# Where the memory projection is normalised in a two-layer decoder trunk: between its last two column groups, or inside the first feed-forward block

## The chip, the cores and the metric

The kernel runs on one core of a Trainium2 chip. The metric is the device time of one execution in microseconds (us). Three executions of the kernel before took 1013.52, 1014.38 and 1016.01 us; the median is 1014.38.

## The reference, cut to what matters

The trunk has two layers over 256 tokens of width 1024. A memory of 256 rows is normalised and projected once, ahead of both layers, and both layers attend to it:

```
mem_kv = rms_norm(mem, mem_norm_g) @ mem_w_kv        # (256, 1024)
mem_k  = mem_kv[..., :512]   # 4 heads of 128, each normalised again in memory_heads
mem_v  = mem_kv[..., 512:]
for i in range(2):
    x = x + 0.5 * swiglu(rms_norm(x, ffn1_norm_g[i]), ffn1_w_in[i], ffn1_w_out[i])
    ... mixer: tokens, and memory_heads(xq, mem_k, mem_v, ...) ...
    x = x + 0.5 * swiglu(rms_norm(x, ffn2_norm_g[i]), ffn2_w_in[i], ffn2_w_out[i])
```

Two facts of `rms_norm` are used. The scale of a row is one number, so it can be applied after the projection as well as before it; the gain is applied before. And nothing reads `mem_k` and `mem_v` until the first mixer, after the whole first feed-forward block.

## The kernel before, in words

Every large product is made in three passes: an operand is split into a rounded high part and the remainder, and `mm3` (L226 to L230) issues high by high, low by high and high by low, each a 128x128x256 matmul on PE. A weight tile of 512 KB arrives by DMA in a `wr` tile (`wtile`, L218, five buffers), ACT casts it to `wh` (L213), and DVE subtracts to get `wl` (L214, eight buffers of each). A tile feeds eight calls of `mm3`, 24 matmuls.

The order of PE and of the DMA queue SP is that of the program text. The text is woven: `Weave` (L61) runs a main generator and side chains, counts modelled PE time (0.328 us for each `mm3`), and resumes a side chain when its stated delay, an entry of `LAT` (L53), has passed. If the main generator yields a condition, the side chain is run at once until the condition holds. ACT, DVE and POOL are ordered by the compiler's scheduler, which may issue an instruction ahead of its place in the text when its inputs are ready; `issue_after` (L466, L490) queues a block behind a given instruction of its engine. At run time each engine takes its instructions in order.

`memory()` (L427) is the first stage. It loads the memory in four pieces, applies the gain and splits them (`mh`, `ml`), and projects in four `Group`s of 256 columns, called here group 0 to group 3: groups 0 and 1 are keys, 2 and 3 values. Each group holds one PSUM bank and takes two weight tiles, called its first and second half.

In the kernel before, the text runs in this order. Behind the casts of group 1, ACT squares the four pieces of memory and DVE adds them (`square`, L279) and folds them (L290, L248). During group 2 the `chain` of the memory's norm follows: on PE a product with a matrix of ones (L308), on DVE two diagonals (L299), on POOL the power that gives `rc` (L313), the row scale. After group 2 the main generator waits in the text for that (`yield norm.ready`), and `head_norm` (L395) normalises the keys of groups 0 and 1, out of their banks: a square on ACT, a reduction on DVE (L401), scalings (L404, L408), a power on POOL (L406), and a product (L410). Then ACT scales the values of group 2 out of their bank into `vM` with `rc` (through `act`, L134), and the residual `x` is prepared for the feed-forward block: `x0.put` (L267) applies gains, splits, squares and sums. Only then come group 3 with its weights, and the scaling of its values. The transposed keys `kT` (L238 on PE, L451 on ACT) follow inside the first feed-forward block (`ffn_in`, L498), as does the product with ones of `x0`'s norm (L308), whose result `rb` the block needs for its first activations (`hidden`).

Of the kernel before, what the change touches and what calls it, by code (L numbers as in the profile page):

```python
# [10 lines left out]
F32 = mybir.dt.float32  # L11
# [3 lines left out]
AF = mybir.ActivationFunctionType  # L15
ALU = mybir.AluOpType
# [3 lines left out]
P = 128  # L20
# [12 lines left out]
def constants():  # L33
# [16 lines left out]

LAT = dict(pieces=1, norm=8.5, mnorm=3.5, x0=17.0, mkeys=7.2, cross=9.5, cross_s=1.5,  # L53
           cross_m=3.7, cross_p=8.7, cross_o=3.0, gates=20.0, scores=2.2, scores_m=8.4, num=6.9, num_r=7.5,
           keys=5.5, keys_d=7.2, query=9.0, head=1.5, head_m=2.5, head_p=9.3, head_o=4.0)

# [42 lines left out]
def tile_trunk(ctx: ExitStack, tc: tile.TileContext, a, out):  # L99
    nc = tc.nc  # L100
    seq = [0]

    def mk(pool, shape, dt, tag):
        seq[0] += 1
        return pool.tile(shape, dt, tag=tag, name=f"{tag}_{seq[0]}")
# [7 lines left out]
    wv = Weave()  # L113
# [19 lines left out]
    def act(*args, **kw):  # L133
        ins = nc.scalar.activation(*args, **kw)  # L134
        if args[2] not in (AF.Copy, AF.Square):
            tabled[0] = ins
# [6 lines left out]
    def unit(dt):  # L143
        return mk(up, [P, 2, T], dt, "u")

    def tmp():
        return mk(tp, [P, 2, T], F32, "t")

    def col():
        return mk(cp, [P, 16], F32, "col")  # L150

    def mo():
        return mk(pb8, [P, 512], F32, "bank")
# [7 lines left out]
    memT = [unit(F32) for _ in range(4)]  # L161
    xT = [unit(F32) for _ in range(4)]
    con = mk(cst, [P, C_END], F32, "con")
# [37 lines left out]
    def g(i):  # L201
        return gcol[:, i:i + 1]


    pieces = [1]
    last = [None]
# [11 lines left out]
    def wtile(src, nk, ncol=256):  # L218
        raw = mk(wrp, [P, nk, ncol], F32, "wr")
        nc.sync.dma_start(raw, src)  # L220
        return split(raw, [P, nk, ncol])

    def wcols(w, c0, kh):
        return wtile(w.rearrange("(k p) f -> p k f", p=P)[:, kh * 4:(kh + 1) * 4, c0:c0 + 256], 4)
# [16 lines left out]
    def split_gain(src, gc, hi, lo):  # L241
        act(hi, src, AF.Copy, scale=gc)
        nc.vector.scalar_tensor_tensor(out=lo, in0=src, scalar=gc, in1=hi.bitcast(F32),
                                       op0=ALU.mult, op1=ALU.subtract)
# [14 lines left out]
    class Norm:  # L259
# [4 lines left out]
            self.done = False  # L264
            self.xT, self.xh, self.xl = [], [], []

        def put(self, xn):  # L267
            c2 = len(self.xT)
            hi, lo = mk(xhp, [P, 2, T], F32R, "xh"), mk(xlp, [P, 2, T], F32R, "xl")
            for m in range(2):  # L270
                split_gain(xn[:, m], g(self.gi + 2 * c2 + m), hi[:, m], lo[:, m])
            self.xh.append(hi)
            self.xl.append(lo)
            self.xT.append(xn)
            self.square(xn, c2 == 0)
            if c2 == 3:
                self.fold()

        def square(self, xn, first):  # L279
            if first:  # L280
# [107 lines left out]
    def head_scales(rc, hd, scaled):  # L388

        c = mk(sp, [P, 4], F32, "qsc")  # L390
        nc.vector.scalar_tensor_tensor(out=c[:, 0:2], in0=rc, scalar=1.0 / hd, in1=rc, op0=ALU.mult, op1=ALU.mult)
        nc.vector.tensor_scalar_mul(c[:, 2:4], rc, hd ** -0.5 if scaled else 1.0)
        return c

    def head_norm(dst, src, n, hsc):  # L395

        hd = src.shape[2] // n
        sq, v, u = tmp(), col(), col()
        sqv = sq[:, :, :n * hd]
        act(sqv, src, AF.Square)  # L400
        nc.vector.tensor_reduce(out=v[:, 0:2 * n].rearrange("p (h m) -> p h m", h=2),  # L401
                                in_=sqv.rearrange("p h (m d) -> p h m d", m=n), axis=AX.X, op=ALU.add)
        for h in range(2):
            nc.vector.tensor_scalar(u[:, n * h:n * h + n], v[:, n * h:n * h + n], hsc[:, h:h + 1], EPS,  # L404
                                    op0=ALU.mult, op1=ALU.add)
        nc.gpsimd.tensor_tensor(out=u[:, 8:8 + 2 * n], in0=u[:, 0:2 * n], in1=mhalf[:, 0:2 * n], op=ALU.pow)  # L406
        for h in range(2):
            nc.vector.tensor_scalar(v[:, 8 + n * h:8 + n * h + n], u[:, 8 + n * h:8 + n * h + n],  # L408
                                    hsc[:, 2 + h:3 + h], None, op0=ALU.mult)
        tt(out=dst.rearrange("p h (m d) -> p h m d", m=n), in0=src.rearrange("p h (m d) -> p h m d", m=n),  # L410
           in1=v[:, 8:8 + 2 * n].rearrange("p (h m) -> p h m", h=2).unsqueeze(3).to_broadcast([P, 2, n, hd]),
           op=ALU.mult)

    def turn(rows):

        ps = mo()
        for m in range(2):
            for h in range(2):
                transpose(ps[:, m * T + h * P:m * T + (h + 1) * P], rows[:, h, m * P:(m + 1) * P])
        return halves(ps)  # L420
# [3 lines left out]
    vM = mk(cst, [P, 2, 512], F32, "vM")  # L424
    x0 = Norm(G_F1)

    def memory():  # L427

        idle = tmp().rearrange("p a b -> p (a b)")[:, :T].bitcast(BF16)
        nc.vector.memset(idle, 0.0)  # L430
        bank = mo()
        for i in range(WARM):
            nc.tensor.matmul(bank, idle[:, :P], idle, start=True, stop=True, skip_group_check=True)
        wkv = a["mem_w_kv"]
        mh, ml, wfirst = [], [], []
        for c2 in range(4):
            nc.sync.dma_start(memT[c2], a["memT"][:, 2 * c2:2 * c2 + 2])
            hi, lo = unit(F32R), unit(F32R)
            for m in range(2):
                split_gain(memT[c2][:, m], g(G_MEM + 2 * c2 + m), hi[:, m], lo[:, m])  # L440
            mh.append(hi)
            ml.append(lo)
            if c2 == 0:
                v = wkv.rearrange("(k p) f -> p k f", p=P)
                wfirst.append([wtile(v[:, k:k + 2, 0:256], 2) for k in (0, 2)])
            if c2 == 2:
                wfirst.append(wcols(wkv, 0, 1))
        norm = Norm(G_MEM, rows=False)

        def keys(gi, kr):  # L450
            nc.scalar.copy(kT[gi], turn(kr))  # L451
            return
            yield

        for gi in range(2):
            gr = Group(wkv, gi * 256, mh, ml, rows=True)
            for kh in range(2):
                if gi == 0 and kh == 0:
                    yield from gr.first_part(wfirst[0])
                else:  # L460
                    yield from gr.part(kh, wfirst[kh] if gi == 0 else None)
            if gi == 0:
                first = gr
                continue
            nc.sync.dma_start(con, a["con"])
            with tc.issue_after(last[0].ins):  # L466
                for c2 in range(4):
                    norm.square(memT[c2], c2 == 0)
            norm.fold()
            wv.spawn(norm.chain(), LAT['mnorm'])  # L470
            gv = Group(wkv, 512, mh, ml, rows=True)
            yield from gv.all()
            for c2 in range(4):
                nc.sync.dma_start(xT[c2], a["xT"][:, 2 * c2:2 * c2 + 2])
            yield norm.ready
            hsc = head_scales(norm.rc, P, False)
            for i, q in enumerate((first, gr)):
                kr = tmp()
                head_norm(kr, q.ps, 2, hsc)
                wv.spawn(keys(i, kr), LAT['mkeys'] + 1.5 * i)  # L480
        for gi in range(2):
            if gi == 0:
                gr = gv
            else:
                gr = Group(wkv, 768, mh, ml, rows=True)
                yield from gr.all()
            for h in range(2):
                act(vM[:, h, gi * 256:(gi + 1) * 256], gr.ps[:, h], AF.Copy, scale=norm.rc[:, h:h + 1])
            if gi == 0:
                with tc.issue_after(last[0].ins):  # L490
                    for c2 in range(4):
                        x0.put(xT[c2])
                wv.spawn(x0.chain(), LAT['x0'])


    KG = [(0, 4), (4, 4), (8, 4), (12, 4), (16, 4), (20, 2)]
# [39 lines left out]
    def ffn(x, w_in, w_out, nxt=None, mid=None):  # L536
# [13 lines left out]
        for c2 in range(4):  # L550
# [25 lines left out]
            else:  # L576
                nxt.put(xn)
        wv.spawn(nxt.chain(), LAT['norm'])

# [15 lines left out]
    def cross_spawn(gr, gi, layer, hsc, ys):  # L595
# [4 lines left out]
        def queries():  # L600
# [4 lines left out]
            for m in range(2):  # L605
                wv.spawn(head(m), LAT['cross_s'] + LAT['cross_m'] * m)
            return
            yield

        def head(m):  # L610
# [12 lines left out]
            tt(out=p, in0=p, in1=c[:, 6:8].unsqueeze(2).to_broadcast([P, 2, T]), op=ALU.mult)  # L623
            yield LAT['cross_p']
            tps = mo()
# [428 lines left out]
```

## Time and profile before

| | before |
|---|---|
| three executions, us | 1013.52, 1014.38, 1016.01 |
| span of the profiled execution, us | 1011.9 |
| median of the executions less that span, us | 2.5 |
| PE, DVE, ACT busy, us | 996.4, 673.3, 524.0 |
| mean granted clock of PE | 0.997 |

The span runs from the first to the last instruction of one profiled execution; no longer time of that execution is given. A row of the trace's timeline has the start, the duration, the engine, the line and operation, the tile written and the tiles read, and in brackets the idle time of the engine before the row with what ended it. PEld is the weight load of PE.

### The profile page before, as it was taken

To read this page: it belongs to the slowest core of one execution; us is meant where nothing else is said; L and a number is where in the kernel's file an instruction comes from. 1 tells how busy PE (TensorE), PEld (TensorE's weight loads), DVE (VectorE), ACT (ScalarE), POOL (GpSimd) and SP (SyncE) were. 2 spreads that over 40 slices of the span, in tenths; PEclk is the share of its full clock that TensorE was granted. 3 is DMA by queue.
4 is the path that set the end of the run, shared out by engine and by line. 5 is a ranking of instruction groups with operands and counts; after the bars stand their busy time and mean duration, and the time that the engine had idled before them with its cause. 6 is when DMAs were issued, how large, how long until landed. Compare 5 with 4: busy or idle time off the path is not lost.

```text
span 1011.9 us, 20587 instructions
## 1 busy us (share of the span) xinstructions
PE 996.4 (98%) x8560; PEld 978.2 (97%) x8560; DVE 673.3 (67%) x1116; ACT 524.0 (52%) x771; POOL 28.5 (3%) x27
## 2 busy tenths in 40 slices
PE   8899999999999999999999999999999999999998
PEld 7899999999999999999999999999987899999998
DVE  6876665668756786666568666656787768666551
ACT  7755444456566564454445444544557665454440
POOL 1100000000100000000000000000121000000000
PEclk9999999999999999999999999999999999999999
DMA  9676666667644566665666666566632247665650
GB/s 310 209 247 189 193 190 180 190 187 204 184 131 138 178 191 199 193 191 178 192 206 201 200 189 192 178 194 199 189 115 81 87 137 222 199 190 183 189 171 22
DMA packets 173205, 182.71 MB, mean 181 GB/s; under 512 B 7124, under 2 KB 168328, under 8 KB 173112
## 3 DMA queue, kind: packets, MB, share of 16 engines
q1 hardware_dynamic: 171872, 179.60, 58.3%
q10 hardware_dynamic: 1016, 1.58, 0.5%
q8 instruction: 67, 1.10, 0.5%
q0 software_dynamic: 224, 0.22, 0.2%
q14 instruction: 26, 0.21, 0.1%
HBM read 180.32 MB, written 1.05 MB: 179 GB/s over the span
## 4 chain that ended last, share of the span: by engine, by line
PE 92%; DVE 4%; ACT 1%; POOL 1%; DMA 1%; issue 0%; SPq 0%; POOLq 0%; ACTq 0%; DVEq 0%
PE bank L227 29%; PE bank L228 29%; PE bank L229 29%; PE bank L233 2%; DVE wl L214 1%; PE bank L238 1%; POOL col L406 1%; ACT u L134 1%; DMA wr<-in_mem_w_kv_dram 1%; PE bank L988 1%; DVE col L401 0%; DVE u L410 0%; DVE u L973 0%; DVE col L957 0%; ACT wh L213 0%
## 5 line engine op out<-in xcount | busy, mean ns | idle before, releaser
L214 DVE TENSOR_TENSOR wl<-wr,wh 128x1024 fp32r<-128x1024 f32 (+1 forms) x347 | 414.7, 1196 | 267.0 <-ACT wh L213 266.2
L213 ACT CAST wh<-wr 128x1024 fp32r<-128x1024 f32 (+1 forms) x347 | 356.9, 1031 | 391.8 <-PE bank L228 367.4
L227 PE MATMUL bank<-xh,wh 128*128 128x256 f32 x1544 | 427.8, 277 | 0.0
L228 PE MATMUL bank<-xl,wh 128*128 128x256 f32 x1544 | 426.4, 276 | 0.0
L229 PE MATMUL bank<-xh,wl 128*128 128x256 f32 x1544 | 426.4, 276 | 0.0
L227 PEld LDWEIGHTS bank<-xh,wh 128*128 128x128 f32 x1544 | 290.0, 188 | 0.1
L228 PEld LDWEIGHTS bank<-xl,wh 128*128 128x128 f32 x1544 | 289.8, 188 | 0.1
L229 PEld LDWEIGHTS bank<-xh,wl 128*128 128x128 f32 x1544 | 289.8, 188 | 0.0
L227 PE MATMUL bank<-u,wh 128*128 128x256 f32 x896 | 249.3, 278 | 0.0
L228 PE MATMUL bank<-u,wh 128*128 128x256 f32 x896 | 247.6, 276 | 0.0
L229 PE MATMUL bank<-u,wl 128*128 128x256 f32 x896 | 247.6, 276 | 0.0
L227 PEld LDWEIGHTS bank<-u,wh 128*128 128x128 f32 x896 | 168.2, 188 | 1.9 <-issue 1.7
L228 PEld LDWEIGHTS bank<-u,wh 128*128 128x128 f32 x896 | 168.3, 188 | 0.1
L229 PEld LDWEIGHTS bank<-u,wl 128*128 128x128 f32 x896 | 168.3, 188 | 0.0
L227 PE MATMUL bank<-wh,xh 128*128 128x256 f32 x208 | 60.3, 290 | 0.0
L228 PE MATMUL bank<-wl,xh 128*128 128x256 f32 x208 | 58.7, 282 | 0.0
L229 PE MATMUL bank<-wh,xl 128*128 128x256 f32 x208 | 58.5, 281 | 0.0
L503 DVE TENSOR_TENSOR t<-bank,rb 128x256 f32<-128x256 f32 x88 | 36.3, 420 | 6.7 <-PE bank L229 6.7
L227 PEld LDWEIGHTS bank<-wh,xh 128*128 128x128 f32 x208 | 39.8, 191 | 0.5 <-issue 0.3
L228 PEld LDWEIGHTS bank<-wl,xh 128*128 128x128 f32 x208 | 39.8, 191 | 0.1
L229 PEld LDWEIGHTS bank<-wh,xl 128*128 128x128 f32 x208 | 39.8, 191 | 0.0
L506 DVE TENSOR_TENSOR t<-t,bank 128x256 f32<-128x256 f32 x88 | 32.7, 413 | 0.0
(182 smaller groups left out, 671.0 us busy)
## 6 DMA issues: line engine op xcount, KB each, us to landing
wr<-in_ffn_w_in_dram SPq DMA_DIRECT2D x176, 512.0 KB, 4.3
wr<-in_ffn_w_out_dram SPq DMA_DIRECT2D x80, 512.0 KB, 3.7
wr<-in_a_w_in_dram SPq DMA_DIRECT2D x28, 512.0 KB, 3.7
wr<-in_b_w_in_dram SPq DMA_DIRECT2D x14, 512.0 KB, 4.6
wr<-in_a_w_out_dram SPq DMA_DIRECT2D x12, 512.0 KB, 3.4
wr<-in_b_w_out_dram SPq DMA_DIRECT2D x12, 512.0 KB, 3.4
wr<-in_ffn_w_out_dram SPq DMA_DIRECT2D x16, 256.0 KB, 2.9
wr<-in_mem_w_kv_dram SPq DMA_DIRECT2D x7, 512.0 KB, 7.8
```

Of the source, the lines that this page charges most:

```text
L134: ins = nc.scalar.activation(*args, **kw)
L213: last[0] = nc.scalar.copy(hi[:, i * n:(i + 1) * n], src[:, i * n:(i + 1) * n])
L214: tt(out=lo[:, i * n:(i + 1) * n], in0=src[:, i * n:(i + 1) * n], in1=hi[:, i * n:(i + 1) * n].bitcast(F32), op=ALU.subtract)
L227: nc.tensor.matmul(ps, wh, xh, start=start, stop=False, skip_group_check=True)
L228: nc.tensor.matmul(ps, wh, xl, start=False, stop=False, skip_group_check=True)
L229: nc.tensor.matmul(ps, wl, xh, start=False, stop=stop, skip_group_check=True)
L233: nc.tensor.matmul(ps, lhsT, rhs, start=start, stop=stop, skip_group_check=True)
L238: nc.tensor.transpose(ps, src, ident[:k, :k])
L406: nc.gpsimd.tensor_tensor(out=u[:, 8:8 + 2 * n], in0=u[:, 0:2 * n], in1=mhalf[:, 0:2 * n], op=ALU.pow)
L503: tt(out=t[:, m], in0=ps[m][:, :T], in1=x.rb, op=ALU.mult)
L506: tt(out=t[:, m], in0=t[:, m], in1=ps[m][:, T:], op=ALU.mult)
L988: nc.tensor.matmul(o[es[e], cs], vr[:, i, js], pTs[e][:, src], start=i == 0, stop=i == 1, skip_group_check=True)
```

## The change: what it does

The text between group 1 and group 3 is emptied. The memory's squares, its norm's chain and the two `head_norm`s leave it; no wait stands there any more. Behind each of the four groups, 4.0 us of modelled PE time after its end, ACT copies the bank unscaled: groups 0 and 1 to two tiles `raw`, groups 2 and 3 into `vM`. The gains and splits of `x` stay behind the casts of group 2, without its squares. After group 3 two chains are started: `sums` makes the squares, the fold and the chain of `x0` (first step 2.5 us into the feed-forward block), and `finish` makes those of the memory (first step at 18.0 us), scales `vM` on DVE in place, normalises the raw keys and starts their transposes. The loads keep their order.

```diff
-LAT = dict(pieces=1, norm=8.5, mnorm=3.5, x0=17.0, mkeys=7.2, ...
+LAT = dict(pieces=1, norm=8.5, mnorm=8.0, mrest=6.0, finish=18.0, raw=4.0, x0=2.5, fold=5.0, mkeys=7.2, ...

-        def put(self, xn):
+        def put(self, xn, square=True):
...
-            self.square(xn, c2 == 0)
-            if c2 == 3:
-                self.fold()
+            if square:
+                self.square(xn, c2 == 0)
+                if c2 == 3:
+                    self.fold()

-        for gi in range(2):
+        def late(raw, gr):
+            nc.scalar.copy(raw, gr.ps)
+            return
+            yield
+
+        def sums():
+            for c2 in range(4):
+                x0.square(xT[c2], c2 == 0)
+                yield 1.5
+            x0.fold()
+            yield LAT['fold']
+            yield from x0.chain()
+
+        def finish(raw):
+            for c2 in range(4):
+                norm.square(memT[c2], c2 == 0)
+                yield 2.0
+            norm.fold()
+            yield LAT['mnorm']
+            yield from norm.chain()
+            yield LAT['mrest']
+            for h in range(2):
+                nc.vector.tensor_scalar(vM[:, h], vM[:, h], norm.rc[:, h:h + 1], None, op0=ALU.mult)
+            hsc = head_scales(norm.rc, P, False)
+            for i in range(2):
+                yield 3.0
+                kr = unit(F32)
+                head_norm(kr, raw[i], 2, hsc)
+                wv.spawn(keys(i, kr), LAT['mkeys'])
+
+        raw = [unit(F32) for _ in range(2)]
+        for gi in range(4):
             gr = Group(wkv, gi * 256, mh, ml, rows=True)
             for kh in range(2):
                 if gi == 0 and kh == 0:
                     yield from gr.first_part(wfirst[0])
                 else:
                     yield from gr.part(kh, wfirst[kh] if gi == 0 else None)
-            if gi == 0:
-                first = gr
-                continue
-            nc.sync.dma_start(con, a["con"])
-            with tc.issue_after(last[0].ins):
+            dst = raw[gi] if gi < 2 else vM[:, :, (gi - 2) * 256:(gi - 1) * 256]
+            wv.spawn(late(dst, gr), LAT['raw'])
+            if gi == 1:
+                nc.sync.dma_start(con, a["con"])
+            if gi == 2:
                 for c2 in range(4):
-                    norm.square(memT[c2], c2 == 0)
-            norm.fold()
-            wv.spawn(norm.chain(), LAT['mnorm'])
-            gv = Group(wkv, 512, mh, ml, rows=True)
-            yield from gv.all()
-            for c2 in range(4):
-                nc.sync.dma_start(xT[c2], a["xT"][:, 2 * c2:2 * c2 + 2])
-            yield norm.ready
-            hsc = head_scales(norm.rc, P, False)
-            for i, q in enumerate((first, gr)):
-                kr = tmp()
-                head_norm(kr, q.ps, 2, hsc)
-                wv.spawn(keys(i, kr), LAT['mkeys'] + 1.5 * i)
-        for gi in range(2):
-            if gi == 0:
-                gr = gv
-            else:
-                gr = Group(wkv, 768, mh, ml, rows=True)
-                yield from gr.all()
-            for h in range(2):
-                act(vM[:, h, gi * 256:(gi + 1) * 256], gr.ps[:, h], AF.Copy, scale=norm.rc[:, h:h + 1])
-            if gi == 0:
+                    nc.sync.dma_start(xT[c2], a["xT"][:, 2 * c2:2 * c2 + 2])
                 with tc.issue_after(last[0].ins):
                     for c2 in range(4):
-                        x0.put(xT[c2])
-                wv.spawn(x0.chain(), LAT['x0'])
+                        x0.put(xT[c2], False)
+        wv.spawn(sums(), LAT['x0'])
+        wv.spawn(finish(raw), LAT['finish'])
 
 
     KG = [(0, 4), (4, 4), (8, 4), (12, 4), (16, 4), (20, 2)]
```

More of the change, by code (lines that the diff above doesn't have):

```diff
@@ L49 @@
 G_MEM, G_F1, G_MIX, G_F2, G_XQ, G_XK, G_AH, G_BQ, G_BK, G_END = 0, 8, 24, 40, 56, 58, 60, 68, 69, 70
-LAT = dict(pieces=1, norm=8.5, mnorm=3.5, x0=17.0, mkeys=7.2, cross=9.5, cross_s=1.5,
+LAT = dict(pieces=1, norm=8.5, mnorm=8.0, mrest=6.0, finish=18.0, raw=4.0, x0=2.5, fold=5.0, mkeys=7.2, cross=9.5, cross_s=1.5,
            cross_m=3.7, cross_p=8.7, cross_o=3.0, gates=20.0, scores=2.2, scores_m=8.4, num=6.9, num_r=7.5,
```

## The prediction

> **What bounds the kernel now.** I read the page's head and its busy table first, then PE's waits, then PE's timeline and the stages around its gaps, then ACT and DVE there.
>
> ```profile
> span 1011.9 us, 20587 instructions
> PE 996.4 (98%) x8560; PEld 978.2 (97%) x8560; DVE 673.3 (67%) x1116; ACT 524.0 (52%) x771; POOL 28.5 (3%) x27
> ```
>
> PE is the bound nearly everywhere: 1011.9 - 996.4 leaves 15.5 us without a matmul. A change that removes no matmul can win only part of these, or of matmuls run at a low clock. PE's waits say where they lie:
>
> ```profile
> PE bank L228 <- DVE wl L214: 3.0, 2, 2.1
> PE bank L227 <- ACT wh L213: 2.3, 2, 2.0
> PE bank L952 <- ACT u L134: 0.9, 1, 0.9
> PE bank L947 <- DVE u L410: 0.8, 1, 0.8
> ```
>
> The two longest waits for weight splits, 2.1 and 2.0 us, are neighbours on PE's timeline, at the start of group 3:
>
> ```profile
> 27.42 0.28 PE L229 MATMUL bank<-wh,u 128*128 128x256 f32 x1
> 29.67 0.39 PE L227 MATMUL bank<-wh,u 128*128 128x256 f32 x1 [1.97 <-ACT wh L213]
> 32.17 0.39 PE L228 MATMUL bank<-wl,u 128*128 128x256 f32 x1 [2.11 <-DVE wl L214]
> 39.34 0.28 PE L227 MATMUL bank<-xh,wh 128*128 128x256 f32 x1
> ```
>
> The row at 39.34 is the first matmul of the feed-forward block (its operand is `xh`). The stage table shows a second cost behind the gap:
>
> ```profile
> core 0: us, PE busy (x) PEld busy (x) DVE busy (x) ACT busy (x) POOL busy (x), PEclk, DMA share, GB/s
> 13.18:27.54 14.36, 14.36 (x121) 14.31 (x121) 11.20 (x22) 10.43 (x19) 0.62 (x1) 1.00 0.97 350
> 27.54:32.17 4.63, 0.55 (x4) 0.19 (x2) 3.42 (x11) 4.32 (x7) 1.45 (x2) 1.00 0.00 0
> 32.59:36.00 3.41, 3.41 (x18) 3.41 (x17) 3.24 (x6) 1.62 (x3) 1.22 (x1) 0.50 0.59 170
> 39.34:62.00 22.66, 22.66 (x201) 22.66 (x200) 20.93 (x29) 14.81 (x19) 0.00 (x0) 1.00 0.95 300
> ```
>
> From 13.18 to 27.54 PE runs unbroken, 121 matmuls in 14.36 us, 0.119 us each. In the gap it runs 4, and the DMA moves nothing. Then for 3.41 us the granted clock is 0.50 and 18 matmuls run where 29 would. Why the gap is there, ACT and DVE tell:
>
> ```profile
> 27.85 0.84 ACT L134 ACTIVATE vM<-bank,rc 128x256 f32<-128x256 f32 x2 [2.69 <-POOL rc L313]
> 28.58 1.99 ACT L213 CAST wh<-wr 128x1024 fp32r<-128x1024 f32 x2
> ```
>
> ```profile
> 26.33 0.29 DVE L299 CUSTOM_DVE_ANT_0 t<-bank,con 128x128 f32<-128x128 f32 x1 [2.33 <-PE bank L308]
> 27.85 0.16 DVE L391 SCALAR_TENSOR_TENSOR qsc<-rc 128x2 f32<-128x2 f32 x1 [0.61 <-POOL rc L313]
> 30.63 0.36 DVE L408 TENSOR_SCALAR col<-col,qsc 128x2 f32<-128x2 f32 x2 [0.91 <-POOL col L406]
> 30.89 1.22 DVE L214 TENSOR_TENSOR wl<-wr,wh 128x1024 fp32r<-128x1024 f32 x1
> 38.14 0.69 DVE L410 TENSOR_TENSOR t<-bank,col 128x512 f32<-128x512 f32 x1
> ```
>
> ACT stands 2.69 us for the row scale `rc`, which the scaling of group 2's values needs, with group 3's casts (28.58) queued behind. DVE stands for PE's product (2.33), for `rc` (0.61) and for the head norm's power (0.91), with group 3's subtraction (30.89) behind. The weights were not late:
>
> ```profile
> 15.12 0.38 SPq L220 DMA_DIRECT2D wr<-in_mem_w_kv_dram  x1
> 21.30 0.37 SPq L220 DMA_DIRECT2D wr<-in_ffn_w_in_dram  x1
> 32.14 0.37 SPq L220 DMA_DIRECT2D wr<-in_ffn_w_in_dram  x1
> ```
>
> ```profile
> wr<-in_mem_w_kv_dram SPq DMA_DIRECT2D x1, 512.0 KB, 8.1
> ```
>
> Group 3's second half was issued at 15.12 and landed 8.1 us later, at 23.2. SP itself stands from 21.30 to 32.14, because the late subtraction frees no `wr` buffer.
>
> **The change part by part.** *The gap.* If PE goes straight from group 2 to group 3, the first feed-forward matmul comes 48 matmuls (two halves of 24) after 27.54: 48 x 0.119 = 5.7, so at 33.24 in place of 39.34. That is 6.1 us: about 1.7 (half of 3.41) for the low clock, the other 4.4 for the waits and the two restarts.
>
> [...]
>
> *Are group 3's splits ready in time?* PE now wants the first half at 27.3 (two matmuls before 27.54, since the memory's product L308 leaves this place; it returns later, so the sum doesn't count it) and the second 24 matmuls, 2.85 us, later, at 30.15. What remains ahead of them is `x0.put` without squares, and up to two raw copies:
>
> ```profile
> L134 ACT ACTIVATE xh<-u,gcol x8: 493/494/506, 20.5 to 24.7; 128x256 fp32r<-128x256 f32 x8
> L243 DVE SCALAR_TENSOR_TENSOR xl<-u,gcol,xh x8: 475/482/486, 21.5 to 29.2; 128x256 fp32r<-128x256 f32 x8
> ```
>
> ```profile
> L213 ACT CAST wh<-wr 128x1024 fp32r<-128x1024 f32 x9 | 9.0, 1052 | 1.8 <-DMA wr<-in_ffn_w_in_dram 1.8
> L286 DVE TENSOR_TENSOR acc<-acc,t 128x512 f32<-128x512 f32 x3 | 2.1, 690 | 0.0
> L451 ACT COPY kT<-bank 128x512 f32<-128x512 f32 x2 | 1.2, 587 | 0.8 <-PE bank L238 0.8
> L401 DVE TENSOR_REDUCE col<-t 128x4 f32<-128x512 f32 x2 | 1.4, 678 | 0.0
> ```
>
> ```profile
> 12.51 0.91 SPq L474 DMA_DIRECT2D u<-in_xT_dram  x2
> ```
>
> ```profile
> u<-in_xT_dram SPq DMA_DIRECT2D x2, 256.0 KB, 7.0
> ```
>
> The last two pieces of `x` are issued from 12.51 and land 7.0 us later, the last by about 20.4. Eight gains of 0.494 on ACT are 4.0 us; even if none begins before 18.5 they end at 22.5. Two raw copies, priced by the copy of a bank of the same size (L451, 0.59), push that to 23.7. A cast of 1.05 and a subtraction of 1.22 (row 30.89) make the first half ready at 26.0; the second, at one subtraction more, at 27.2. Both come before PE wants them, by 1.3 and 2.9 us; without the copies the first margin is 2.5. So the whole 6.1 is taken. The copies are also the waits that the change adds: each waits on ACT for its group's last matmul, with the next casts queued behind. The text places it 4 us after that matmul, and behind it PE has the splits already made to live on.
>
> *The loads.* The moved work issues no DMA, and the order on SP is unchanged. The subtractions of group 3 at about 26 free the `wr` buffers that SP awaited until 32.14, so the feed-forward loads resume some 6 us earlier. That is as much as PE moves, and no load becomes late.
>
> *The work moved into the feed-forward block.* On ACT, four copies of 0.59 replace the four scalings of `vM`, half a bank each (0.84 for two): 0.7 us more, in an engine that is busy 14.81 of 22.66 us there. ACT feeds PE in time at that share. POOL gets the memory's powers, and is idle there (x0 in the same row). The moved DVE work is larger. By the row for L286, three sums of 0.69; two fold steps of half that size, 0.35 each; two diagonals of 0.29; two scalings of `vM`, not in the trace in this form, bounded by 0.35 (half of a 128x512 operation) and 0.69 (all of it), taken at 0.69 each; and for each head norm a reduction 0.68, four small scalings 0.7 (0.36 for two) and a product 0.69. That is 2.1 + 0.7 + 0.6 + 1.4 + 4.1 = 8.9 us. It lies between about 53 and 83 us: the chain starts 18 us of modelled time behind group 3, its last head norm stands at 18 + 8 + 8 + 6 + 3 + 3 = 46, and a modelled 0.328 is really 3 x 0.119 = 0.357. The room:
>
> ```profile
> 60.00:70.00 10.00, 10.00 (x91) 10.00 (x90) 8.24 (x13) 6.11 (x8) 0.00 (x0) 1.00 0.67 205
> 70.00:80.00 10.00, 10.00 (x90) 10.00 (x90) 6.05 (x10) 5.26 (x6) 0.00 (x0) 1.00 0.59 182
> 80.00:90.00 10.00, 10.00 (x91) 10.00 (x90) 6.76 (x9) 4.58 (x6) 0.00 (x0) 1.00 0.67 204
> ```
>
> DVE idles 1.8 + 4.0 + 3.2 = 9.0 us there, and may use up several of the eight buffered splits before PE notices. I cost it at nothing; without that cover it would be up to 8.9 us.
>
> *The new joins on PE.* Each product with ones and each set of transposes is placed in PE's fixed order, so if its operand is late, all matmuls behind it wait. Four joins are re-timed: `x0`'s product, the memory's product, two key transposes. Before, none of these held PE. The nearest rows that did are the mixer's waits of 0.9 and 0.8 at L952 and L947. The bounds are therefore 0 and 4 x 0.9 = 3.6. As nothing waited there, there is nothing to gain. I take 0.4, half of one such wait, since the stated delays leave 5 to 8 us for each.
>
> *The sum.* 6.1 - 0.4 = 5.7. The span would be 1011.9 - 5.7 = 1006.2. The median of the three runs lies 2.5 above the span; the same 2.5 gives **1008.7 us**, or 1014.38 - 5.7. From the fastest run, 1.6 above the span, it would be 1007.8. Everything later is PE's own steady work, so the gain carries to the end.
>
> **The rivals.**
>
> *The change does not do what it says: group 3's splits still come late (1013.7).* The scheduler may issue work ahead of its place in the text. It does so now:
>
> ```profile
> 1.26 0.07 DVE L826 MEMSET v<- 128x2 f32 x2
> 7.46 0.17 DVE L196 TENSOR_SCALAR nsink<-sink 128x16 f32<-128x16 f32 x1 [4.51 <-DMA sink<-in_b_sinks_dram]
> ```
>
> Both belong to the mixers, and one cost DVE 4.51 us. Nothing holds the new squares behind a cast any more. If the raw copy of group 2, which waits for its last matmul at 27.5, is put ahead of the casts, the first half is ready at 27.7 + 0.6 + 1.05 + 1.22 = 30.6, not 27.3. PE waits 3.3, the low clock takes 1.7 and the joins 0.4, and 0.7 is kept: 1013.7. If both sums (2.1 + 0.7 = 2.8 us of DVE each) run ahead of the subtraction, it is ready at 26.0 + 5.6 = 31.6, and the time is 1014.7; with one set alone 28.8, a wait of 1.5 at full clock, and 1010.2. Against it: the text places all of these behind group 3's casts.
>
> *The low clock is not in the median run (1010.4).* The waits alone give 4.4 - 0.4 = 4.0. For it: the clock row stands for one execution only, and the three times spread by 2.5 us. [...]
>
> *Slower: the head norms inside the block are too slow for their transposes (about 1018).* Before, the two head norms took from 27.85 to 38.14 + 0.69, 11.0 us, with weight splits between their steps. Now each has 7.2 modelled, 7.8 real us to its transposes. If each took 11.0, PE would wait 3.2 twice, each with a low clock of 1.7: 9.8 lost, 3.7 net, 1018.1. The gain is spent when each wait reaches 1.35 (2 x 3.05 = 6.1), a head norm of 9.2; from 2.9, or 10.7, on the change is slower by over 0.3%. Against it: two norms shared those 11.0 us, and stood in queues with group 3's starved splits.
>
> **How the numbers follow.** A measurement of this kernel can tell about 0.3%, 3 us, from no change: faster is below 1011.3, slower above 1017.4. Forecast 0.60; low clock absent 0.14; splits late 0.18, a quarter of it still below 1011.3; slower 0.08. Faster is 0.60 + 0.14 + 0.04 = 0.78, same 0.14, slower 0.08. The range starts at 1006.0: with joins that cost nothing (1008.3) and the 1.6 of the fastest run it would be 1007.4, and the three times differ by more than 1.4 among themselves. It ends at 1013.0, between the late splits' 1010.2 and 1014.7; left out are the slower case and some 0.11 of the late ones, 0.19 in all.
>
> **What would show it.** Right: no wait for `wh` or `wl` at group 3; the first `xh` matmul near 33; clock 1.00 from 32 to 36; `wr` loads at about 26; no idle time before the products with ones and the transposes. Wrong: squares of memory or `x` ahead of group 3's casts on ACT; a copy from a bank there with idle time put down to PE; a row of PE with `[... <-DVE ...]` between 45 and 90 us.

## The result, and the profile after

Eight executions of the changed kernel took 1010.63 to 1013.5 us, median 1012.8, beside a median of 1014.48 of the kernel before. The ratio, formed from all these executions (the two medians alone give 0.9983), is 0.9978, 95% interval 0.9968 to 0.9989: faster by 1.7 us between the medians, where 5.7 was forecast. The profiled execution took 1010.63 and is at the lower end; its span of 1008.8 stands against 1011.9.

```profile
span 1008.8 us, 20591 instructions
PE 994.7 (99%) x8560; PEld 976.4 (97%) x8560; DVE 673.5 (67%) x1118; ACT 525.2 (52%) x771; POOL 28.3 (3%) x27
```

PE's waits for weight splits are smaller than before, but not gone (columns as before: total, times, longest):

```profile
PE bank L227 <- ACT wh L213: 2.1, 2, 1.6
PE bank L228 <- DVE wl L214: 1.8, 2, 0.9
```

PE's timeline shows that they stand at the same place, the start of group 3:

```profile
27.15 0.28 PE L229 MATMUL bank<-wh,u 128*128 128x256 f32 x1
29.05 0.39 PE L227 MATMUL bank<-wh,u 128*128 128x256 f32 x1 [1.62 <-ACT wh L213]
30.31 0.38 PE L228 MATMUL bank<-wl,u 128*128 128x256 f32 x1 [0.87 <-DVE wl L214]
35.95 0.29 PE L227 MATMUL bank<-xh,wh 128*128 128x256 f32 x1
```

The stage table (same columns as before) has the gap and group 3 behind it, at full clock in this execution, 48 matmuls in 5.64 us:

```profile
27.27:30.31 3.04, 0.55 (x4) 0.19 (x2) 1.28 (x2) 2.85 (x4) 0.00 (x0) 1.00 0.00 1
30.31:35.95 5.64, 5.64 (x48) 5.64 (x49) 5.64 (x7) 4.99 (x7) 0.00 (x0) 1.00 0.66 193
```

The first feed-forward matmul comes at 35.95, 3.4 earlier than before (39.34), where 33 was expected. ACT's timeline says why:

```profile
16.16 0.59 ACT L457 COPY u<-bank 128x512 f32<-128x512 f32 x1 [0.97 <-PE bank L229]
16.64 2.00 ACT L213 CAST wh<-wr 128x1024 fp32r<-128x1024 f32 x2
21.81 0.59 ACT L457 COPY u<-bank 128x512 f32<-128x512 f32 x1 [3.17 <-PE bank L229]
22.30 3.31 ACT L134 ACTIVATE xh<-u,gcol 128x256 fp32r<-128x256 f32 x8
25.51 0.62 ACT L134 ACTIVATE acc<-u 128x512 f32<-128x512 f32 x1
27.46 0.59 ACT L457 COPY vM<-bank 128x512 f32<-128x512 f32 x1 [1.33 <-PE bank L229]
27.95 1.05 ACT L213 CAST wh<-wr 128x1024 fp32r<-128x1024 f32 x1
```

The raw copies (L457) stand in ACT's queue ahead of work that PE will need. Group 1's copy stands where the text has it, behind group 2's casts and ahead of the gains of `x`; but ACT runs ahead of PE, reaches it at 18.6 and waits 3.17 us for PE's last matmul of group 1, while the gains, whose inputs had landed by about 20.5 (issued by 13.40, 7.0 us to landing), stand behind it. Group 2's copy was issued ahead of its place in the text, which is behind group 3's casts; it waits 1.33 us for group 2, and group 3's first cast stands behind it. DVE is starved by the same queue, 2.75 us before the gains' remainders and 2.90 before group 3's subtraction, which ends at 30.25:

```profile
22.84 3.29 DVE L243 SCALAR_TENSOR_TENSOR xl<-u,gcol,xh 128x256 fp32r<-128x256 f32 x8 [2.75 <-ACT xh L134]
29.02 1.23 DVE L214 TENSOR_TENSOR wl<-wr,wh 128x1024 fp32r<-128x1024 f32 x1 [2.90 <-ACT wh L213]
```

SP again stands for the `wr` buffers, from 20.12 to 30.28 in place of 32.14. The rest went as the prediction expected: in the feed-forward block neither the products with ones nor the key transposes held PE, and DVE carried the moved work at 27.2 us busy of 30.

```profile
60.00:70.00 10.00, 10.00 (x91) 10.00 (x90) 9.49 (x18) 7.86 (x12) 0.00 (x0) 1.00 0.57 174
70.00:80.00 10.00, 10.00 (x91) 10.00 (x90) 9.16 (x21) 5.67 (x8) 0.72 (x1) 1.00 0.65 195
80.00:90.00 10.00, 10.00 (x90) 10.00 (x90) 8.56 (x21) 5.48 (x6) 3.49 (x3) 1.00 0.53 162
```

### The profile page after: what moved, and what is told of

Same layout as the page of the kernel before. It is cut to its first block, busy times and chain, and to the rows that moved or that the text cites. A ratio compares the mean times of both kernels' runs of the same rounds, so it can differ in the third digit from the quotient of the medians.

```text
span 1008.8 us, 20591 instructions
## 1 busy us (share of the span) xinstructions
PE 994.7 (99%) x8560; PEld 976.4 (97%) x8560; DVE 673.5 (67%) x1118; ACT 525.2 (52%) x771; POOL 28.3 (3%) x27
## 4 chain that ended last, share of the span: by engine, by line
PE 90%; DVE 4%; ACT 2%; DMA 1%; POOL 1%; issue 1%; SPq 0%; POOLq 0%; ACTq 0%; DVEq 0%
PE bank L229 29%; PE bank L227 29%; PE bank L228 29%; PE bank L233 2%; ACT u L134 1%; DVE wl L214 1%; POOL col L407 1%; PE bank L238 1%; DMA wr<-in_ffn_w_in_dram 1%; DMA wr<-in_mem_w_kv_dram 1%; ACT wh L213 1%; DVE u L985 0%; DVE col L969 0%; PE bank L1000 0%; DVE col L402 0%
```

## The experiments

Theory A: the copies' place on ACT, each waiting for PE ahead of work that PE needs, keeps the gap. Its rival, theory B: the gains, the squares or the weights' landing do. Theory C is on the spread of the times: the half clock follows a gap in some executions only.

**Group 2's copy held** behind group 3's casts.

```diff
         def late(raw, gr):
-            nc.scalar.copy(raw, gr.ps)
+            with tc.issue_after(last[0].ins):
+                nc.scalar.copy(raw, gr.ps)
```

> The raw copies are queued behind the last weight cast made when they are written; on ACT only group 2's copy moves, from ahead of group 3's casts to behind them. Theory A (group 3 is late because raw copies that wait for PE stand in ACT's queue ahead of its casts): group 1's copy still ends at 22.3 and the gains of x at 25.5, two squares follow, so group 3's first cast ends near 27.6 and its subtraction near 28.9. PE loses about 1.5 us in place of 2.9, the first xh matmul is near 34.5 in place of 35.95, and the time of a run at full clock is about 1009.2 in place of 1010.6. Theory B (the gains of x, the squares or the landing of the weights make group 3 late, whatever the copies do): the first xh matmul stays at 35.9 and the times stay as they are.

Median 1010.8 (1009.3 to 1011.2), ratio to before 0.9965 (0.9951 to 0.9978). On ACT group 1's copy stays where it was, which shows that it already stood at its place in the text, and group 2's copy now follows group 3's casts:

```profile
22.05 0.59 ACT L458 COPY u<-bank 128x512 f32<-128x512 f32 x1 [3.17 <-PE bank L229]
28.26 1.03 ACT L213 CAST wh<-wr 128x1024 fp32r<-128x1024 f32 x1
29.19 0.58 ACT L458 COPY vM<-bank 128x512 f32<-128x512 f32 x1
```

PE's timeline of the profiled execution:

```profile
27.88 0.39 PE L227 MATMUL bank<-wh,u 128*128 128x256 f32 x1 [0.21 <-ACT wh L213]
29.14 0.38 PE L228 MATMUL bank<-wl,u 128*128 128x256 f32 x1 [0.87 <-DVE wl L214]
34.77 0.28 PE L227 MATMUL bank<-xh,wh 128*128 128x256 f32 x1
```

The two waits fell from 1.62 + 0.87 to 0.21 + 0.87, the first `xh` matmul from 35.95 to 34.77. One copy of 0.59 us, moved behind two casts, was worth 1.2 us, and this execution, at full clock, took 1009.3 where 1009.2 was expected: theory A. What is left lies behind group 1's copy, as the next run shows.

**All copies held.** In addition to the edit above:

```diff
-... finish=18.0, raw=4.0, x0=2.5, ...
+... finish=18.0, raw=9.0, x0=2.5, ...
```

> The raw copies are written 9.0 in place of 4.0 us of modelled time behind their groups, and queued behind the last cast made by then, so that group 1's copy too stands behind group 3's casts. Two squares of x still stand ahead of group 3's first cast. Theory A: gains of x run from about 19 to 22.5, the first cast ends near 24.6, the subtraction near 26; PE goes from group 2 to group 3 without a wait, the first xh matmul is at 32.9, the time 1007.6 (1010.6 - 3.0), and the runs spread less, since there is no gap that could bring a low clock. Theory B: a wait of 1 us or more stays at group 3 and the time stays above 1009.5.

Median 1009.29 (1007.55 to 1009.95), ratio 0.9945 (0.9933 to 0.9958). ACT's timeline:

```profile
18.96 3.31 ACT L134 ACTIVATE xh<-u,gcol 128x256 fp32r<-128x256 f32 x8
23.22 1.04 ACT L213 CAST wh<-wr 128x1024 fp32r<-128x1024 f32 x1
```

The gains run at 18.96 in place of 22.30, group 3's first cast at 23.22 in place of 27.95, and PE waits for nothing between 14 and 60 us. Two squares of `x` still stand between gains and cast, and cost PE nothing. The first `xh` matmul of this profile is at 34.60, not at 32.9, because this execution had a stretch at half clock from 13.36 to 16.78, long before group 3:

```profile
13.36:16.78 3.42, 3.42 (x16) 3.42 (x17) 3.23 (x5) 2.30 (x3) 0.00 (x0) 0.50 1.08 388
34.60 0.28 PE L227 MATMUL bank<-xh,wh 128*128 128x256 f32 x1
```

Less the 1.5 that such a stretch costs (below), 34.60 is 33.1. The expected 1007.6 was reached by the quicker executions (1007.55, 1007.85), not by the median; that the spread would shrink was wrong, since the start has waits of its own (PE 0.60 and 0.88 us, and 12 matmuls in the 3.41 us ahead of 13.36).

**Copies and squares held.** In addition:

```diff
-                x0.square(xT[c2], c2 == 0)
+                with tc.issue_after(last[0].ins):
+                    x0.square(xT[c2], c2 == 0)
```

> As the run with all copies held, and the squares of x too are queued behind the last cast. Theory A: nothing more to win, first xh matmul at 32.9, time within 0.5 us of that run, 1007.6. If the squares ahead of group 3's casts are the cause instead, this one alone has no wait at group 3.

Median 1007.92 (1007.3 to 1009.56), ratio 0.9941 (0.9928 to 0.9953), no wait of PE between 14 and 60 us, and the first `xh` matmul at 32.27:

```profile
32.27 0.28 PE L227 MATMUL bank<-xh,wh 128*128 128x256 f32 x1
```

Its interval overlaps that of the run before, so the squares' place is not shown to matter; the copies' is. This is what the prediction had priced: 1007.9 measured, 1008.7 forecast, span 1005.7 against 1006.2.

**The residual's squares alone** moved, the memory left as before.

```diff
-                        x0.put(xT[c2])
-                wv.spawn(x0.chain(), LAT['x0'])
+                        x0.put(xT[c2], False)
+        wv.spawn(sums(), 2.5)
```

> The kernel before with only the residual's squares, fold and chain moved into the first feed-forward block, as in the change; the memory is finished between groups 2 and 3 as before. Theory A (what holds group 3 is a wait for PE or for the memory's norm ahead of its casts): nothing won, the first xh matmul at about 39, the time 1014.2 within 0.7. If the squares of x are what makes group 3 late, the gap shrinks by their 2 us and the time is about 1012.

Median 1014.82, ratio 1.0007 (0.9998 to 1.0016): nothing won. PE waits 1.97 and 2.68 us at group 3, where the kernel before waits 1.97 and 2.11, and the first `xh` matmul is at 39.97, where about 39 was expected. So the residual's squares were not what held group 3.

**The memory alone** moved, the residual's squares back in `put`.

```diff
-                        x0.put(xT[c2], False)
-        wv.spawn(sums(), LAT['x0'])
+                        x0.put(xT[c2])
+        wv.spawn(x0.chain(), LAT['x0'] + 5.0 + 6.0)
```

> The changed kernel, but with the residual's squares back in x0.put, ahead of group 3's casts, and its chain started at about the same modelled time. ACT's order then has group 1's copy (ends 22.3 as it waits for PE), eight gains, four squares, group 3's casts, and only then group 2's copy. Theory A: gains and squares take 22.3 + 3.3 + 2.5 = 28.1, the first subtraction is done at 30.4, PE loses about 3 us as in the changed kernel, first xh matmul at 36.1, time 1010.7 to 1013. If the squares cost their whole 2.5 us on top of the changed kernel's gap, the first xh matmul is at 38.4 and the time about 1014.

Median 1012.57 (1010.82 to 1014.01), ratio 0.9982 (0.9973 to 0.9991), as the whole change. Its profile has the half clock at the start, from 13.43 to 16.84, which shifts all times below by some 1.5 (1.55 was measured for a stretch, see the changed kernel again); on ACT:

```profile
23.59 0.59 ACT L457 COPY u<-bank 128x512 f32<-128x512 f32 x1 [3.17 <-PE bank L229]
29.37 1.98 ACT L213 CAST wh<-wr 128x1024 fp32r<-128x1024 f32 x2
31.55 0.57 ACT L457 COPY vM<-bank 128x512 f32<-128x512 f32 x1
```

Here group 2's copy stands behind group 3's casts, but the squares stand ahead, and PE's waits are 1.25 and 1.15 us, the first `xh` matmul at 37.62, as expected with the 1.5 added. So the residual's part of the change was worth nothing as long as a copy held ACT up: what it freed, group 2's copy took.

**Matmuls on zeros in the gap** of the changed kernel (`idle` gets a tile of its own).

```diff
             gr = Group(wkv, gi * 256, mh, ml, rows=True)
+            if gi == 3:
+                for _ in range(8):
+                    nc.tensor.matmul(bank, idle[:, :P], idle, start=True, stop=True, ...)
```

> The changed kernel with eight 128x512 bf16 matmuls on zeros (0.21 us each at full clock, 1.7 us) in PE's order ahead of group 3, inside its gap of 2.9 us; the results of these matmuls are not used. Theory C (the changed kernel's runs spread from 1010.6 to 1013.5 because the gap brings a stretch of half clock in some executions): the gap stays, the first xh matmul stays near 36.0, but the slower runs go, and the median falls from 1012.8 to about 1010.8. Rival (the spread has another cause): median and spread as in the changed kernel, or up to 0.3 us slower.

Median 1010.75, four of five executions at 1010.53 to 1010.76 and one at 1012.26. The first `xh` matmul stays late, at 36.03. The median is as expected, but the interval of the ratio (0.9955 to 0.9980) overlaps that of the changed kernel. The granted clock speaks for theory C too: its mean was 0.998 or more in all five executions, and in only six of the changed kernel's twenty (eight above, twelve below). The one at 1012.26 had 0.998 as well; a mean does not say where in the execution a stretch lies.

**The changed kernel again**, unaltered.

> The changed kernel once more, unaltered, for a second profile and more times beside the kernel before. Theory C (half clock behind its gap in some executions and not in others): times fall in two groups, 1010.6 where the gap brings no half clock and 1012 to 1013.5 where it does, and the profile, if of the upper group, shows a stretch of clock 0.50 within 5 us of 30.3 or, from the gap at the start, of 13.2. Rival: one group, or a slow profile without such a stretch before 60 us.

> The changed kernel, unaltered, for one more profile. The two profiles so far show half clock at 13.4 (one of them) and at 743 (both), and none behind the gap at group 3. [...]

> [...]

The first gave ten times of 1010.92 to 1014.01, median 1012.07, ratio 0.9975 (0.9966 to 0.9984); the other two runs took 1012.37 and 1012.26. In the profiles of the first and the last the half clock begins at 13.37 and 13.60, and the first `xh` matmul is at 37.49 and 37.60. In the second it begins behind the gap; its stage table, 3.41 us before and 3.41 from there:

```profile
26.91:30.32 3.41, 0.96 (x6) 0.55 (x5) 1.24 (x2) 2.80 (x4) 0.00 (x0) 1.00 0.01 3
30.32:33.73 3.41, 3.37 (x16) 3.37 (x16) 3.41 (x5) 3.41 (x6) 0.00 (x0) 0.50 0.51 160
```

and its timeline has:

```profile
37.50 0.29 PE L227 MATMUL bank<-xh,wh 128*128 128x256 f32 x1
```

That is 1.55 later than in the profile at full clock. Theory C holds in its first part: an execution pays some 1.5 us at the start, at group 3, or, as in the changed kernel's first profile, at neither, and which it is differs. Of the twenty executions, the six with a mean granted clock of 0.998 took 1010.63 to 1011.98 us, the fourteen with less 1011.97 to 1014.01. That times fall in two sharp groups was wrong; between 1010.6 and 1014.0 they lie nearly everywhere.

**The kernel before with matmuls on zeros**, nine ahead of group 3.

```diff
                 gr = Group(wkv, 768, mh, ml, rows=True)
+                for _ in range(9):
+                    nc.tensor.matmul(bank, idle[:, :P], idle, start=True, stop=True, ...)
```

> The kernel before, with nine matmuls on zeros ahead of group 3, inside the first part of its gap (1.9 of the 2.1 us before the first matmul of group 3); their results are not used. Theory C: the gap stays 4.6 us long, but the half clock behind it goes in most executions: 1014.2 - 1.7 = 1012.5. Rival (the half clock in the profile of before was not typical): the time stays at 1014.2.

No gain is shown: median 1013.94, ratio 0.9997 (0.9988 to 1.0005). Its profile still has the half clock, from 32.03; 2.11 us of the gap stayed empty, and the 3.41 us ahead of the stretch held 6 matmuls. But five of its eleven executions have a mean granted clock of 0.998, which none of the 51 executions of the kernel before whose clock is known reaches (0.993 to 0.997), and these five are its quickest, 1012.30 to 1013.91 us. So theory C fits about half of the executions, not most.

**Held, with matmuls on zeros in both gaps left**, on top of the kernel with copies and squares held.

```diff
+                    if gi == 0:
+                        warm(bank, 5)
                     yield from gr.part(kh, wfirst[kh] if gi == 0 else None)
...
             s = mo()
+            if layer == 1 and gi == 1 and m == 0:
+                warm(s, 10)
```

> The kernel with copies and squares held, with matmuls on zeros in the two gaps of PE that are left: five in the start, ahead of the second half of group 0, ten in the second layer's cross attention, ahead of the first scores of its second pair of heads (0.21 us each at full clock, 1.1 and 2.1 us); their results are not used. Theory C (each gap of about 2 us can bring 3.4 us of half clock, depending on the execution): all executions at full clock, time 1006.0 to 1006.5 in each, against 1007.3 to 1009.6. Rival (the spread has another cause): median 1007.9 and the same spread; or the idle matmuls delay the real ones, and it is slower.

Median 1008.28 (1007.98 to 1008.45). The spread fell from 2.3 to 0.5 us, but the expected 1006.0 to 1006.5 was missed by 2. In the mixer PE's timeline shows where it went, with the idle matmuls first:

```profile
738.84 1.13 PE L233 MATMUL bank<-kT,u 128*128 128x256 f32 x4 [0.22 <-ACT u L134]
742.64 1.04 PE L238 MATMUL bank<-con,u 128*128 128x128 f32 x8
748.19 1.13 PE L233 MATMUL bank<-t,vM 128*128 128x256 f32 x4 [1.80 <-ACT t L652]
```

and without them, where matmuls that took 0.28 us before took 0.42 each from 740.36 to 743.35 (mean clock 0.97 from 720 to 770, 1.00 with them):

```profile
738.75 1.13 PE L233 MATMUL bank<-kT,u 128*128 128x256 f32 x4 [2.38 <-ACT u L134]
744.07 1.04 PE L238 MATMUL bank<-con,u 128*128 128x128 f32 x8
747.83 1.13 PE L233 MATMUL bank<-t,vM 128*128 128x256 f32 x4
```

At full clock PE reaches the transposes 1.4 us sooner, then waits 1.80 us for ACT. The chain through ACT and DVE sets the time there, so half clock at that place cost nothing in these two executions. So there was nothing to win there, though the expectation lay 0.8 to 1.3 below the quickest execution without idle matmuls (1007.3). Besides, the run with idle matmuls lost time of its own: further on PE waits 1.41 us for ACT in place of 0.93, and the next weight matmul starts at 759.07 in place of 758.23, though the two profiles were only 0.09 apart at 738.8. Why ACT is later there stays open.

**Held, with the start's five alone.**

```diff
-            if layer == 1 and gi == 1 and m == 0:
-                warm(s, 10)
```

> The kernel with copies and squares held, with the five matmuls on zeros in the gap at the start alone, and none in the mixer; their results are not used. The half clock in the mixer costs nothing by the last profiles (PE only waits there later instead), so the theory expects what the best executions without the idle matmuls had, 1007.3, in nearly every execution: median 1007.5, spread under 0.7. Rival (the half clock in the mixer makes the spread): median 1007.9 or more and a spread of 2.

Median 1007.76 (1007.43 to 1008.62), ratio 0.9930 (0.9916 to 0.9943). The spread is 1.2, between the two expectations, and the half clock does not explain it: the slowest execution is the profiled one, and its mean granted clock is 0.999, where one stretch of 3.41 us at half clock in its span of 1006.8 would alone make 0.998. It and the kernel with copies and squares held beat both kernels; their intervals overlap.

## Why the prediction was wrong, point by point

**The step that failed** is "Are group 3's splits ready in time?", in its sentences on the raw copies: "Two raw copies, priced by the copy of a bank of the same size (L451, 0.59)", and "The text places it 4 us after that matmul". The copies take 0.59 each, but each is also a wait for PE, which the sum put at nothing. The 4 us are counted in modelled PE time; among ACT's instructions they fix a place, not a time. ACT ran ahead of PE and stood at the copies of groups 0 and 1, at their places in the text, for 0.97 and 3.17 us. Group 2's copy was issued ahead of its place as well, and ACT stood there for 1.33. The first split was ready at 30.25, not 26.0. What the prediction named as a sign of being wrong, a copy from a bank ahead of the casts with idle time put down to PE, is what ACT's timeline shows. For group 2's copy, L826 and L196, quoted as early issues, were the warning: a prediction that lets the scheduler issue early in one paragraph must not read the order from the text in another.

**The rival that came true** is "the change does not do what it says", by the route it names, group 2's copy ahead of the casts. It put the split at 30.6 (measured 30.25), PE's wait at 3.3 (3.0 from 27.27 to 30.31), and the time at 1013.7 with the half clock, thus 1012.0 without; measured were 1012.8 in the median and 1010.63 in the profiled execution, which has no half clock there. It was given 0.18. It left out that group 1's copy holds up the gains as well, worth another 1.1 us: holding group 2's copy alone left 1.08 us of waits, holding both left none. That 1012.8 lies inside the stated range, 1006.0 to 1013.0, is no merit of the forecast: the upper end was set by this rival. By the prediction's own line at 1011.3 the change counts as the same, which was given 0.14.

**The gap.** The 6.1 us were right: with copies and squares held the span fell by 6.2, 1011.9 to 1005.7. That it fits so closely is in part luck. The first `xh` matmul came 7.1 earlier (32.27 for 39.34), since this execution ran the matmuls ahead of it at the quicker of two paces, one every 0.113 us in place of 0.118 (last section), and 0.9 of that was lost again behind it, at the slower one. With all copies held, at the slower pace (one every 0.118 us) as in the kernel before, 34.60 less the 1.55 of its half clock is 33.05, where 33.24 was forecast. Of the 1.7 for the half clock, 1.5 was measured per stretch, and it is not paid in every execution. The same kernel had its first recorded stretch at 13.37, 13.60, 30.32 or only at 742.55 us. The runs speak against the rival "low clock not in the median run": all three profiles with the gap of before, those of the kernel before, of the residual's squares alone and with idle matmuls, have the half clock behind it (from 32.59, 32.51 and 32.03), and no execution of the kernel before whose clock is known has more than 0.997.

**The loads.** The loads were expected to resume at about 26. With copies and squares held SP stood only from 19.83 to 24.69; in the changed kernel it stood until 30.28, since the subtraction that frees the buffer was late.

**The moved work and the joins.** Both right. DVE took the moved work without holding up PE, and the four joins cost 0 where 0.4 was taken. The scalings of `vM` took 0.88 together, 0.44 each, in the bounds of 0.35 and 0.69. The 8.9 us leave out the residual's own sums and folds, which moved too (2.8 by the prediction's prices); they ran mostly beside group 3, where the stage table has DVE busy for the whole 5.64 us, and PE still waited for nothing. The slower rival fell. On DVE and PE:

```profile
80.43 0.68 DVE L402 TENSOR_REDUCE col<-t 128x4 f32<-128x512 f32 x1
88.15 1.29 DVE L411 TENSOR_TENSOR u<-u,col 128x512 f32<-128x512 f32 x2
```

```profile
94.90 0.60 PE L238 MATMUL bank<-con,u 128*128 128x128 f32 x4
```

Both head norms together took 9.0 us, from the first reduction to the end of the second product at 89.44, and PE came for the keys 5.5 us later, without a wait.

**The time around the span** is 1.7 to 1.9 us in every execution that shows both (1010.63 and 1008.8), not 2.5: the median of before less the span of one profile mixed two executions. With 1.8 the forecast span of 1006.2 gives 1008.0.

## What to carry to other kernels

An instruction that takes a result from another engine is a wait at the place where the queue has it (here up to 3.17 us for a copy of 0.59); before it is priced by its duration, find what will stand behind it in the queue, and when its engine will get there. A delay in the text that is counted in one engine's time says nothing of when another engine arrives, and where a scheduler orders the queue, the order has to be stated (here one held line, worth 1.2 us, and a later place, worth the rest). And when a change removes one wait from a shared queue, list the next one in that queue with its time: here it was some 3 us of the 6 on offer.

## What the runs showed of the hardware

The stretches of half clock shown in the tables lasted 3.41 or 3.42 us and held 16 to 18 matmuls, where 29 would run at 0.119 us each. The 3.41 us ahead of them held 4 matmuls in the kernel before (29.18 to 32.59), 6 in the second run of the changed kernel again (26.91 to 30.32), 12 with all copies held (9.95 to 13.36), and 13 in the first run of the changed kernel again, where the longest single wait was 0.88 us:

```profile
9.96:13.37 3.41, 2.09 (x13) 1.49 (x12) 2.64 (x5) 2.50 (x4) 0.00 (x0) 1.00 1.08 389
13.37:16.78 3.41, 3.41 (x17) 3.41 (x17) 3.03 (x5) 1.45 (x2) 0.00 (x0) 0.50 1.08 387
```

So no single wait as long as the stretch stood ahead of this one. Nor was the gap at group 3 always followed by half clock: in the changed kernel's first profile it held 4 matmuls from 27.27 to 30.31, and the 48 behind it ran at clock 1.00. What decides it is not shown here.

At clock 1.00 matmuls also ran at two paces. In the profile with copies and squares held:

```profile
20.00:32.00 12.00, 12.00 (x108) 12.00 (x107) 10.91 (x16) 10.66 (x17) 0.00 (x0) 1.00 1.00 338
34.00:51.00 17.00, 17.00 (x147) 17.00 (x145) 12.26 (x13) 10.41 (x12) 0.00 (x0) 1.00 0.93 303
55.00:72.00 17.00, 17.00 (x152) 17.00 (x151) 16.45 (x31) 11.89 (x18) 0.00 (x0) 1.00 0.53 163
```

That is 0.111, 0.116 and 0.112 us each; the counts take in a few matmuls at the edges, and from start to start it is 0.113 between 25.81 and 31.82 and 0.118 between 32.39 and 44.88. In the kernel before the slower pace lasts until the first key transposes at 42.17: 0.118 from 40.75 to 42.05, 0.114 from 42.73 to 43.53. Over 17 us the slower pace costs 0.7, an estimate from 0.113 and 0.118, which is the size of the differences between the held kernels. What switches it stays open.
